# Turn-by-turn row halves for the scores and transposes of an RWKV-7 scan on Trainium2

## The chip, the cores and the metric

The kernel runs on one core of one Trainium2 chip. The metric is the device time of one execution in microseconds (us), as a median over runs. All arithmetic is in float32; the large products split each operand in a high and a low part, so that one dense product is three matrix instructions.

## What is computed

The reference is a decoder trunk of two layers on 1024 tokens of width 1024. Layer 0 mixes tokens with a gated linear recurrence, layer 1 with RWKV-7; behind each mixer stand a SwiGLU feed-forward part (22 tiles of 128 hidden units) and a gated embedding. The change lies in the RWKV-7 layer, whose heart is a state of 64 by 64 for each of 16 heads:

```python
def step(S, inp):
    r_t, w_t, k_t, v_t, a_t, b_t = inp
    sa = jnp.einsum('bhvk,bhk->bhv', S, a_t)
    S = S * w_t[:, :, None, :] + sa[..., None] * b_t[:, :, None, :] + v_t[..., None] * k_t[:, :, None, :]
    y = jnp.einsum('bhvk,bhk->bhv', S, r_t)
    return S, y
```

followed by a norm of each head's output, a bonus term, a gate and the output projection.

## The kernel before

The tokens are worked in two halves of 512. The recurrence above is done in chunks of 64 tokens (eight chunks per half), for pairs of heads: head 0 of a pair lies in partitions 0 to 63 (`E`), head 1 in 64 to 127 (`O`). There are 16 pair-halves (8 pairs, 2 halves of tokens), and two pairs make a group `G`, 8 groups in all.

`scan()` is made of four generators that run beside each other and beside the dense products of other stages:

- `stage1` builds, for each pair-half, the tiles `BK` (keys), `ZL` and `RB`; it forms the **scores** (`sc`) of four chunks at a time, so two rounds per pair-half, and then the **transposes** of `BK` into `BKt` (`bkt`, line 1079). A score product has 64 rows of contraction, 128 output partitions and 128 columns; a round has four of them for each head. VectorE masks each head's scores out of PSUM in three instructions (L1056 to L1058). ScalarE copies each head's transposes (L1082).
- `inverse` inverts the triangular matrices of a group (tiles `w`, `n`, `u`, `v`), by products on blocks that alternate between the upper and the lower partitions.
- `stage2` walks over the chunks of a group: `zu` and `y` products, of which those that read `z` and `V` (L1207) and those into `y` (L1223) also alternate between the two halves of the partitions, each half with its own half of the output partitions.
- `norm2` norms the outputs of a group, two pairs one behind the other (`bsum` at L1247, `yv` at L1254), loads the gate, and stores `o` (L1264). The two pairs of a group share two buffers of the tag `t3` (`bon` and `sq`): the second pair's loads wait until the first pair is through with them.

TensorE's order is fixed by hand while the scan runs. Every matrix instruction adds its estimated time to `self.clock` (`mm`, L114). After each dense product `tick` (L125) looks whether a generator may go on: each has yielded how long its operands will take (times `slack`, 3 in the first part and 2.5 at the end), whether it takes a PSUM bank, and what must have been traced before. The scan's rounds share `BANKS = 2` banks of tag `b`; `big` (L967) hands them out by turns, and `evac` notes at which planned time a bank will be free. Before the change each head's round takes one bank and is a step of its own, with a planned pause between the steps.

Where the dense products run out, `until` lets the scan run alone (L1352 to L1368): before the output projection of pairs 6 and 7 of the first half (`K.until(lambda: K.n2[3])`, L1360), and at the end, before the room of the scan is given to other tiles:

```python
    K.ffn(1, (0,), None, FA)
    K.until(lambda: not K.streams)
    c.close()
    extra(ctx)
```

The dense products have the names `pps` (projections), `pg` and `pu` (gate and up of the feed-forward part), `ops` (output projections: `ops<-hid` of the feed-forward part, `ops<-on` of the mixer). Their weights come by DMA into `raw`, are rounded by ScalarE (L237) and their rest is formed by GpSimd (L238), both into `whl`.

Of the kernel before, what the change touches and what calls it, by code (L numbers as in the profile page):

```python
# [25 lines left out]
# the plan of TensorE's order beside the scan: PSUM banks of the scan's rounds, the factor on  # L26
# its latencies with the pause behind each of its steps (ns) for either half, and how far the evacuations move ahead of what was traced before them.
# [26 lines left out]
class Part:  # L54
    def __init__(self, gen):
        self.gen, self.need = gen, (0.0, False, None)


class Kern:
# [47 lines left out]
    def ahead(self, n):  # L107
        """ahead of the n instructions traced before, where the scan runs beside dense products."""
        return self.tc.high_priority(n) if self.region else nullcontext()
# [11 lines left out]
    def ready(self, st):  # L121
        lat, bank, cond = st.need
        return (cond is None or cond()) and max(lat, self.bank_free[self.bank_n % BANKS] if bank else 0.0)

    def tick(self, wait=False):  # L125
        """lets each part of the scan whose operands should be there by now issue its next products."""
        while self.streams and (wait or self.clock >= self.hold):
            for st in self.streams:
                t = self.ready(st)
                if t is not False and t <= self.clock:  # L130
                    self.step(st)
                    break
            else:
                return
# [12 lines left out]
    def until(self, cond):  # L147
        """the scan alone until cond holds."""
        self.tick(True)
        while not cond():  # L150
            ts = [t for t in map(self.ready, self.streams) if t is not False]
            self.clock = max(self.clock, min(ts))
            self.tick(True)

    def pause(self, lat):
        """the dense products wait for other engines."""
        if self.streams:
            end = self.clock + lat
            while self.clock < end and self.streams:
                self.tick(True)  # L160
                ts = [t for t in map(self.ready, self.streams) if t is not False]
                self.clock = min([end] + [t for t in ts if t > self.clock])
# [6 lines left out]
    def ln_exp(self):  # L169
        """loads the one table that has both Ln and Exp, behind what ScalarE got up to here."""  # L170
        self.tc.keep_in_program_order(self.nc.scalar.preload_act_table_set("natural_log_exp_and_others"))

    def sigmoid(self, out, x, bias=None, nbias=None):
        """beside the scan without another table: exp(-ln(1 + exp(-x)))."""
        nc = self.nc
        if not self.region:
            nc.scalar.activation(out, x, AF.Sigmoid, **({} if bias is None else {"bias": bias}))
        else:
            nc.scalar.activation(out, x, AF.Exp, scale=-1.0, **({} if nbias is None else {"bias": nbias}))
            nc.scalar.activation(out, out, AF.Ln, bias=self.ones[: out.shape[0], 0:1])  # L180
            nc.scalar.activation(out, out, AF.Exp, scale=-1.0)

# [9 lines left out]
    def ps(self, nm):  # L192
        """a PSUM bank of a dense product."""
        if self.pe is not None:
            self.npe += 1
            if self.npe % 8 % 3:
                return self.pe.tile([128, TH], F32, tag="mm", name=nm, bufs=5)
        return self.pp.tile([128, TH], F32, tag="mm", name=nm, bufs=3)

    def xq(self, nm, ext=None):  # L200
        """8 KB: two k-tiles of half the tokens, hi and lo."""
        if ext is None:
            return self.xp.tile([128, 2, 2, TH], F32R, tag="xq", name=nm, bufs=6)
        return self.ep.tile([128, 2, 2, TH], F32R, tag=ext, name=nm, bufs={"xb": 4, "hid": 2}[ext])

    def ring(self, tag, shape, dt, bufs, more):
        """a slot of a ring, of the longer one while there is room for it."""
# [6 lines left out]
    def load_w(self, src, n, scale=None):  # L214
        """src: [128, n] float32 in DRAM -> f(part, a, b): columns a..b of the hi (0) or lo (1) part.

        scale: (factors [128, n / s / i, i], s), one for each s columns.
        """
# [26 lines left out]
    def mm3(self, *products):  # L245
        """(PSUM, list of (whi, wlo, xhi, xlo)): sums of products; of several ones with the first halves of the lists ahead."""
# [15 lines left out]
    def lead(self, tiles, n):  # L262
        """the first n tiles, whose operands may be on their way, beside each other; then one by one."""
        n = n if self.region else 1
        return [tiles[:n]] + [[i] for i in tiles[n:]]

    def halves(self, src, scale, xs, t, rows=128):
        """as wx for all k, with each 512 columns of the weights loaded when their products come."""
# [62 lines left out]
    def raw_x(self, k, t, gname, gi):  # L331
        """a tile of h times the gains; what divides by the norm stands behind the products with it."""
# [12 lines left out]
    def raw_norm(self, t, keep=True):  # L345
        """the norm for it, when the next products have begun."""
        def norm():
            self.rn[t] = self.rstd(t, self.acc[t] if keep else self.t2("rstd"))

        self.items = [lambda: None, norm]  # L350
# [9 lines left out]
    def order(self, n, tail, ts):  # L360
        """(tile, half): both halves of the first tiles, then half after half of the last ones."""
# [9 lines left out]
    def out_proj(self, wload, nk, hid, ts, bias=None, last=False, nxt=None, raw=None):  # L371
        """h += w @ hid; hid(k, t) -> (hi, lo)."""
# [25 lines left out]
    def hawk_consts(self):  # L398
# [15 lines left out]
        # 8 softplus(-lam) = 8 max(-lam, 0) + 16 atanh(e / (2 + e)); half of it, with either sign  # L414
# [17 lines left out]
    def hawk_tile(self, c, ts=(0, 1)):  # L432
# [6 lines left out]
        for t in ts:  # L439
# [23 lines left out]
            # sigmoid(x) = (1 + tanh(x / 2)) / 2  # L463
# [151 lines left out]
    def ple_last(self, l, t, ph, n=KD - 1):  # L615
        """the last tile of all, half after half of its columns, each up to the final norm."""
# [73 lines left out]
    def pre_rwkv(self, t):  # L690
        """keeps h in DRAM and normalizes it in place, its gains left to the mixes."""
# [15 lines left out]
    def xn_b(self, k0, k1):  # L707
        """the normalized tokens of half 1."""
# [7 lines left out]
    def half_b(self):  # L716
        """half 1 in the place of half 0."""
# [21 lines left out]
    def rwkv_proj(self, t):  # L739
# [13 lines left out]
        def shifted(cur, prev, p0, n, i):  # L753
            """cur + prev of the token before, normalized: products with (1 - mu) w and with mu w."""
# [83 lines left out]
        def unit(n, k):  # L838
            """k * k_k, of length 1 in each head."""
# [92 lines left out]
    def scan(self):  # L932
        """the scan of both halves, as parts that run beside each other and beside dense products.

        Each part yields (time until its next products' operands are there, whether these take a
        bank, what else has to be traced before them).
        """
# [36 lines left out]
        def evac():  # L974
            """called behind a round's products."""
# [13 lines left out]
        def stage1():  # L989
# [15 lines left out]
            for P, (t, g, jj) in enumerate(order):  # L1005
# [19 lines left out]
                # the slots of AB, ZL and RB are those of three pairs before  # L1025
# [3 lines left out]
                for c4 in range(0, NC, 4):  # L1029
# [18 lines left out]
                    yield 1500, True, None  # L1048
                    for hh, me, ot in HV:
                        ps = big("sc", 1700).rearrange("p (c s) -> p c s", c=4)  # L1050
                        for c in range(4):
                            self.mm(ps[:, c, :], BK[me, c4 + c, :, :].rearrange("p i s -> p (i s)"), zl[me, hh, c, :])
                        evac()
                        m3 = mask.unsqueeze(1).to_broadcast([128, 4, 128])
                        with self.ahead(AHEAD_S1):
# [3 lines left out]
                        if hh == 0:  # L1059
                            yield 0, True, None  # L1060
                yield 0, True, (lambda: (G == 0 or inv[G - 1] >= 1) and (old < 0 or s2[old] == NC))
# [13 lines left out]
                for hh, me, ot in HV:  # L1075
                    ps = c3(big("bkt", 800))
                    for c in range(NC):
                        nc.tensor.transpose(ps[:, c, :], BK[me, c, :, :].rearrange("p i s -> p (i s)"), ident[me])
                    self.clock += NC * 54
                    evac()  # L1080
                    with self.ahead(AHEAD_S1):
                        nc.scalar.copy(BKt[:, :, hh, :], ps)  # L1082
                    if hh == 0:
                        yield 0, True, None
# [12 lines left out]
        def inverse():  # L1097
            """(1 - A)^-1, A strictly triangular: blocks of 16 by substitution, then their products."""
# [189 lines left out]
    def rwkv_out(self, t, k0, k1, last=False, nxt=None, raw=None):  # L1288
        """h += w_o @ what tiles k0..k1 of the heads give."""
# [161 lines left out]
```

## Time and profile before

| what | us |
|---|---|
| median of 3 runs | 3109.62 |
| lowest and highest run | 3108.08, 3117.14 |
| span of the profiled execution | 3107.1 |
| TensorE busy in it | 2961.4 (95%) |
| VectorE, ScalarE, GpSimd busy | 1668.7, 1439.2, 1272.7 |

The profile gives the profiled execution no other time than its span, from its first to its last instruction; the median of the runs lies 2.5 us above it. The scan's products lie between 1131 and 2470 us. One float32 matrix instruction of the program shows as two records in the trace, each behind a record of its weight load; a transpose shows as one record. In the program order a row `sc ... x4` is therefore eight records.

### The profile page before, as it was taken

How to read it: one execution, taken by the hardware profiler on the slowest of the kernel's cores; microseconds unless marked ns; L12 is line 12 of the kernel's file. 1: busy time of each engine (PE TensorE's matmuls, PEld its weight loads, DVE VectorE, ACT ScalarE, POOL GpSimd, SP SyncE). 2: the span in 40 equal slices, each digit the busy share in tenths (PEclk: the TensorE clock that was granted, in tenths of full speed). 3: DMA queues.
4: the chain of work that ended last, by engine and by line, in shares of the span. 5: the costliest groups of instructions: out<-in, count | busy, mean ns of one | idle time of the engine just before them, and what ended most of it. 6: DMA issues, size and time to landing. Idle time of an engine off the chain costs nothing. (4 is left out here: it accounts for less than half of the span.)

```text
span 3107.1 us, 45858 instructions
## 1 busy us (share of the span) xinstructions
PE 2961.4 (95%) x16904; PEld 2290.3 (74%) x16904; DVE 1668.7 (54%) x2950; ACT 1439.2 (46%) x2565; POOL 1272.7 (41%) x1080
## 2 busy tenths in 40 slices
PE   5999999999999999999999899999999999999998
PEld 4777778888776777777776667777767777888886
DVE  8766671111563266565667665767866456222145
ACT  5564752222555443434455774454344445322244
POOL 5111134444445444443434334434333355544445
PEclk9999999999998999999999999999999999999999
DMA  3211123333335464333332457423323262333323
GB/s 122 64 36 53 50 82 102 95 95 95 99 124 176 157 193 129 87 110 89 100 108 89 141 174 212 132 85 111 101 88 101 70 185 87 104 96 95 95 81 109
DMA packets 223968, 336.04 MB, mean 108 GB/s; under 512 B 56960, under 2 KB 75136, under 8 KB 223744
## 3 DMA queue, kind: packets, MB, share of 16 engines
q1 hardware_dynamic: 223456, 332.75, 35.0%
q8 instruction: 133, 2.18, 0.3%
q14 instruction: 91, 0.75, 0.1%
q10 hardware_dynamic: 288, 0.37, 0.0%
HBM read 278.24 MB, written 54.79 MB: 107 GB/s over the span
## 5 line engine op out<-in xcount | busy, mean ns | idle before, releaser
L238 POOL TENSOR_TENSOR whl<-raw,whl 128x512 fp32r<-128x512 f32 (+2 forms) x818 | 1053.4, 1293 | 1441.8 <-ACT whl L237 1366.9
L237 ACT CAST whl<-raw 128x512 fp32r<-128x512 f32 (+2 forms) x818 | 482.2, 593 | 845.4 <-PE ops L115 228.7
L115 PE MATMUL ops<-hid,whl 128*128 128x512 f32 x2112 | 528.3, 403 | 19.2 <-ACT hid L288 7.8
L115 PE MATMUL pg<-xn,whl 128*128 128x512 f32 (+1 forms) x2184 | 526.0, 394 | 4.0 <-ACT whl L237 3.1
L115 PEld LDWEIGHTS ops<-hid,whl 128*128 128x128 f32 x2112 | 394.7, 191 | 120.5 <-DVE hid L289 12.9
L115 PEld LDWEIGHTS pg<-xn,whl 128*128 128x128 f32 x2184 | 405.8, 188 | 98.2 <-issue 4.4
L115 PE MATMUL pu<-xn,whl 128*128 128x512 f32 x1584 | 385.6, 396 | 2.7 <-ACT xn L288 1.4
L115 PEld LDWEIGHTS pu<-xn,whl 128*128 128x128 f32 x1584 | 296.0, 189 | 71.3 <-DVE xn L289 2.0
L115 PE MATMUL pps<-mix,whl 128*128 128x512 f32 x1152 | 301.8, 412 | 12.0 <-ACT mix L288 8.3
L389 DVE TENSOR_TENSOR h<-h,ops 128x512 f32<-128x512 f32 x256 | 174.1, 685 | 212.5 <-PE ops L115 210.6
L554 DVE TENSOR_TENSOR sg<-sg,pu 128x512 f32<-128x512 f32 x88 | 60.3, 685 | 404.4 <-PE pu L115 404.0
L115 PEld LDWEIGHTS pps<-mix,whl 128*128 128x128 f32 x1152 | 217.1, 193 | 75.6 <-ACT mix L288 10.3
L115 PE MATMUL pg<-raw,whl 128*128 128x512 f32 x720 | 199.7, 416 | 0.0
L115 PEld LDWEIGHTS pg<-raw,whl 128*128 128x128 f32 x720 | 133.7, 192 | 34.7 <-issue 4.1
L240 POOL TENSOR_SCALAR whl<-raw 128x512 fp32r<-128x512 f32 (+2 forms) x84 | 58.5, 701 | 216.4 <-PE rps L115 74.6
L115 PE MATMUL pu<-raw,whl 128*128 128x512 f32 x528 | 140.9, 406 | 0.0
L115 PE MATMUL rps<-xn,whl 128*128 128x512 f32 x480 | 123.0, 404 | 16.4 <-ACT xn L288 10.4
L115 PEld LDWEIGHTS rps<-xn,whl 128*128 128x128 f32 x480 | 91.9, 193 | 42.5 <-issue 12.0
L115 PE MATMUL gps<-xn,whl 128*128 128x512 f32 x480 | 118.4, 401 | 0.0
L115 PE MATMUL ops<-m,whl 128*128 128x512 f32 x480 | 114.4, 396 | 0.8 <-ACT m L288 0.8
L115 PEld LDWEIGHTS pu<-raw,whl 128*128 128x128 f32 x528 | 96.1, 188 | 23.4 <-issue 1.9
L115 PEld LDWEIGHTS gps<-xn,whl 128*128 128x128 f32 x480 | 92.4, 193 | 21.6 <-issue 0.5
(277 smaller groups left out, 4006.7 us busy)
## 6 DMA issues: line engine op xcount, KB each, us to landing
raw<-in_ffn_in SPq DMA_DIRECT2D x352, 256.0 KB, 2.6
raw<-in_ffn_out SPq DMA_DIRECT2D x152, 256.0 KB, 2.7
raw<-in_rkv SPq DMA_DIRECT2D x96, 256.0 KB, 3.1
raw<-in_ple_gate SPq DMA_DIRECT2D x64, 256.0 KB, 2.6
raw<-in_w_in SPq DMA_DIRECT2D x48, 256.0 KB, 2.8
h<-h SPq DMA_DIRECT2D x32, 256.0 KB, 3.3
raw<-in_ffn_out SPq DMA_DIRECT2D x48, 128.0 KB, 2.1
raw<-in_w_o SPq DMA_DIRECT2D x24, 256.0 KB, 2.7
```

Source lines behind the costliest of these rows:

```text
L115: self.nc.tensor.matmul(out, lhsT=lhsT, rhs=rhs, start=start, stop=stop)
L237: nc.scalar.copy(hl[:rows, 0, :w], raw[:rows, :w])
L238: nc.gpsimd.tensor_sub(hl[:rows, 1, :w], raw[:rows, :w], hl[:rows, 0, :w].bitcast(F32))
L240: nc.gpsimd.tensor_scalar(hl[:rows, 0, :w], raw[:rows, :w], 1.0, 0.0, ALU.mult, ALU.add)
L389: nc.vector.tensor_add(hs, hs, ps)
L554: nc.vector.tensor_mul(sg, sg, pu)
```

## The change

A generator may now ask for two banks at once: `need` holds a number, and `ready` waits until both of the next banks are free by the plan. In a round of scores both heads' banks are taken together, and the products go chunk by chunk, head 0 on the upper 64 rows of TensorE into one bank, head 1 on the lower 64 rows into the other. The plan's clock takes 200 ns off for each second product. Six VectorE instructions follow, in the order of before. The transposes are treated alike: sixteen in a burst, head by head in turn, into two banks, then two copies on ScalarE. No instruction is added or taken away. (Comment lines that go with it are left out.)

```diff
 class Part:
     def __init__(self, gen):
-        self.gen, self.need = gen, (0.0, False, None)
+        self.gen, self.need = gen, (0.0, 0, None)
...
     def ready(self, st):
         lat, bank, cond = st.need
-        return (cond is None or cond()) and max(lat, self.bank_free[self.bank_n % BANKS] if bank else 0.0)
+        return (cond is None or cond()) and max([lat] + [self.bank_free[(self.bank_n + i) % BANKS] for i in range(int(bank))])
...
-                    yield 1500, True, None
-                    for hh, me, ot in HV:
-                        ps = big("sc", 1700).rearrange("p (c s) -> p c s", c=4)
-                        for c in range(4):
-                            self.mm(ps[:, c, :], BK[me, c4 + c, :, :].rearrange("p i s -> p (i s)"), zl[me, hh, c, :])
-                        evac()
-                        m3 = mask.unsqueeze(1).to_broadcast([128, 4, 128])
-                        with self.ahead(AHEAD_S1):
+                    yield 1500, 2, None
+
+                    pss = [big("sc", e).rearrange("p (c s) -> p c s", c=4) for e in (1700, 3400)]
+                    for c in range(4):
+                        for hh, me, ot in HV:
+                            self.mm(pss[hh][:, c, :], BK[me, c4 + c, :, :].rearrange("p i s -> p (i s)"), zl[me, hh, c, :])
+                            if hh:
+                                self.clock -= 200
+                    evac()
+                    evac()
+                    m3 = mask.unsqueeze(1).to_broadcast([128, 4, 128])
+                    with self.ahead(AHEAD_S1):
+                        for hh, me, ot in HV:
+                            ps = pss[hh]
                             nc.vector.tensor_mul(AB[me, cs, :], ps[me, :, 0:64], m3[me, :, 0:64])
                             nc.vector.tensor_mul(rb[me], ps[me, :, 64:128], m3[me, :, 64:128])
                             nc.vector.tensor_mul(zl[ot, hh], ps[ot], m3[ot])
-                        if hh == 0:
-                            yield 0, True, None
-                yield 0, True, (lambda: (G == 0 or inv[G - 1] >= 1) and (old < 0 or s2[old] == NC))
+                yield 0, 2, (lambda: (G == 0 or inv[G - 1] >= 1) and (old < 0 or s2[old] == NC))
...
-                for hh, me, ot in HV:
-                    ps = c3(big("bkt", 800))
-                    for c in range(NC):
-                        nc.tensor.transpose(ps[:, c, :], BK[me, c, :, :].rearrange("p i s -> p (i s)"), ident[me])
-                    self.clock += NC * 54
-                    evac()
-                    with self.ahead(AHEAD_S1):
-                        nc.scalar.copy(BKt[:, :, hh, :], ps)
-                    if hh == 0:
-                        yield 0, True, None
+                pss = [c3(big("bkt", e)) for e in (800, 1400)]
+                for c in range(NC):
+                    for hh, me, ot in HV:
+                        nc.tensor.transpose(pss[hh][:, c, :], BK[me, c, :, :].rearrange("p i s -> p (i s)"), ident[me])
+                self.clock += NC * 60
+                evac()
+                evac()
+                with self.ahead(AHEAD_S1):
+                    for hh in range(2):
+                        nc.scalar.copy(BKt[:, :, hh, :], pss[hh])
```

Since the plan sets TensorE's order, the scan's steps move to other places among the dense products. Three places follow. The first is the start of the scan on TensorE: the scores of the first pair among the projections `pps` (and `vtr`, transposes of values). Before:

```order
L115 MATMUL pps<-mix,whl 128x512 x15
L115 MATMUL sc<-ZL,BK 128x128 x4
L115 MATMUL pps<-mix,whl 128x512 x6
L115 MATMUL sc<-ZL,BK 128x128 x4
L115 MATMUL pps<-mix,whl 128x512 x3
L115 MATMUL vtr<-cst,o 128x128 x4
L115 MATMUL pps<-mix,whl 128x512 x23
L115 MATMUL sc<-ZL,BK 128x128 x4
```

With the change:

```order
L115 MATMUL pps<-mix,whl 128x512 x15
L115 MATMUL sc<-ZL,BK 128x128 x8
L115 MATMUL pps<-mix,whl 128x512 x9
L115 MATMUL vtr<-cst,o 128x128 x4
L115 MATMUL pps<-mix,whl 128x512 x24
L115 MATMUL vtr<-cst,o 128x128 x4
L115 MATMUL pps<-mix,whl 128x512 x7
L115 MATMUL sc<-ZL,BK 128x128 x8
```

The four bursts of a pair-half's scores are two now, and the second comes 40 dense products and 8 `vtr` behind the first.

The second place is the output projection of the first half (`ops<-on`), on TensorE. Its first 144 products take heads 0 to 11 and its last 48 the heads 12 to 15, for each tile of outputs three products with pair 6 and then three with pair 7 (heads 14 and 15), which comes out of the last `yv` of group 3. Before, that `yv` stands in the middle of the projections `pps`, and `ops<-on` begins 128 products `pps` later:

```order
L115 MATMUL pps<-mix,whl 128x512 x8
L1078 MATMUL bkt<-cst,BK 128x64 x8
L115 MATMUL pps<-mix,whl 128x512 x6
L115 MATMUL yv<-v,cst 128x512
L115 MATMUL pps<-mix,whl 128x512 x8
L115 MATMUL vtr<-cst,o 128x128 x8
L115 MATMUL pps<-mix,whl 128x512 x24
```

With the change:

```order
L115 MATMUL yv<-v,cst 128x512
L115 MATMUL ops<-on,whl 128x512 x13
L115 MATMUL sc<-ZL,BK 128x128 x8
L115 MATMUL ops<-on,whl 128x512 x48
L1082 MATMUL bkt<-cst,BK 128x64 x16
L115 MATMUL ops<-on,whl 128x512 x18
L115 MATMUL bsum<-b,cst 128x512
L115 MATMUL ops<-on,whl 128x512 x26
L115 MATMUL yv<-v,cst 128x512
L115 MATMUL ops<-on,whl 128x512 x61
```

Group 3's last `yv` now stands behind 105 of the 144 products, with 39 of them left before the 48 (the 61 are these 39 and 22 of the 48).

The third place is the end of the scan: on TensorE, the last `y` and the norms of group 7. Before:

```order
L115 MATMUL y<-RB,SV 64x64 x4
L115 MATMUL pg<-raw,whl 128x512 x11
L115 MATMUL pu<-raw,whl 128x512 x24
L115 MATMUL pg<-raw,whl 128x512 x2
L115 MATMUL bsum<-b,cst 128x512
L115 MATMUL pg<-raw,whl 128x512 x22
L115 MATMUL yv<-v,cst 128x512
L115 MATMUL pu<-raw,whl 128x512 x24
L115 MATMUL pg<-raw,whl 128x512 x24
L115 MATMUL pu<-raw,whl 128x512 x12
L115 MATMUL bsum<-b,cst 128x512
```

With the change:

```order
L115 MATMUL ops<-hid,whl 128x512
L115 MATMUL zu_8241<-z,V 64x64 x2
L115 MATMUL zu_8242<-z,V 64x64 x2
L115 MATMUL y<-RB,SV 64x64 x4
L115 MATMUL bsum<-b,cst 128x512
L115 MATMUL yv<-v,cst 128x512
L115 MATMUL bsum<-b,cst 128x512
L115 MATMUL yv<-v,cst 128x512
L115 MATMUL pu<-raw,whl 128x512 x24
L115 MATMUL pg<-raw,whl 128x512 x48
```

The dense products of the stage `FA` are used up before the scan is done, so its last six steps stand behind each other with nothing between. On the DMA queue of SyncE the weights of the `pg` products then stand behind the last store of the scan (these rows are of the change):

```order
L1264 DMA v<-g_390 128x512
L1268 DMA o_406<-ys 128x512
L226 DMA raw<-in_ffn_in 128x512 x2
L1281 DMA h_22146<-h_248 128x512
L1281 DMA h_22146<-h_250 128x512
```

Before, that store was issued while `ops<-hid` of the stage `FA` still ran on TensorE.

## Rows read from the trace of the kernel before

**Rows 1.** The page's first line.

```profile
span 3107.1 us, 45858 instructions
```

**Rows 2.** Windows, the scan: length, five engines' busy us (count), PEclk, DMA, GB/s.

```profile
1131.00:2470.00 1339.00, 1277.25 (x9796) 954.07 (x9795) 878.44 (x1876) 649.11 (x1322) 528.41 (x428) 0.97 0.38 116
```

**Rows 3.** By tile, the scores: duration ns min/median/max, first and last start.

```profile
L115 PE MATMUL sc<-ZL,BK x512: 271/272/579, 1131.9 to 2360.0; 64*128 64x128 f32 x171
L1056 DVE TENSOR_TENSOR AB<-sc,cst x64: 392/419/429, 1133.1 to 2360.3; 64x256 f32<-64x256 f32 x64
...
L1058 DVE TENSOR_TENSOR ZL<-sc,cst x64: 676/689/695, 1133.8 to 2361.1; 64x512 f32<-64x512 f32 x64
```

**Rows 4.** By tile, the transposes.

```profile
L1078 PE MATMUL bkt<-cst,BK x256: 221/222/274, 1149.8 to 2365.9; 64*128 64x64 f32 x128
```

**Rows 5.** Timeline, TensorE: start us, us, instruction; two bursts of scores.

```profile
1131.88 1.16 PE L115 MATMUL sc<-ZL,BK 64*128 64x128 f32 x8
1132.96 1.66 PE L115 MATMUL pps<-mix,whl 128*128 128x512 f32 x6
1134.56 1.16 PE L115 MATMUL sc<-ZL,BK 64*128 64x128 f32 x8
```

**Rows 6.** Timeline, TensorE: two bursts of transposes.

```profile
1149.79 0.71 PE L1078 MATMUL bkt<-cst,BK 64*128 64x64 f32 x8
1150.42 2.11 PE L115 MATMUL pps<-mix,whl 128*128 128x512 f32 x8
1152.47 0.71 PE L1078 MATMUL bkt<-cst,BK 64*128 64x64 f32 x8
```

**Rows 7.** Timeline, TensorE: a long run of dense products.

```profile
2504.67 20.10 PE L115 MATMUL ops<-hid,whl 128*128 128x512 f32 x86
```

**Rows 8.** Timeline of 60 ns: the first two records of an alternating burst.

```profile
1277.45 0.27 PE L115 MATMUL zu<-z,V 64*64 64x64 f32 x2
```

**Rows 9.** Timeline of 150 ns: the first two records of one score product.

```profile
1131.88 0.48 PE L115 MATMUL sc<-ZL,BK 64*128 64x128 f32 x2
```

**Rows 10.** Timeline, all engines: the last steps of the scan.

```profile
2466.62 0.45 PE L115 MATMUL zu<-z,V 64*64 64x64 f32 x8
...
2467.24 0.37 DVE L1210 COPY SV<-zu 64x64 f32<-64x64 f32 x2 [0.25 <-ACT SV L1209]
...
2498.33 1.02 PE L115 MATMUL bsum<-b,cst 128*128 128x512 f32 x2
...
2499.39 0.69 DVE L1250 SCALAR_TENSOR_TENSOR b<-bsum,v 128x512 f32<-128x512 f32 x1
...
2500.11 0.63 ACT L1251 ACTIVATE v<-ys 128x512 f32<-128x512 f32 x1 [0.41 <-DVE b L1250]
...
2504.22 1.02 PE L115 MATMUL yv<-v,cst 128*128 128x512 f32 x2
...
2510.04 0.76 DVE L1263 TENSOR_TENSOR ys<-ys,v 128x512 f32<-128x512 f32 x1 [0.34 <-DMA v<-g]
...
2512.40 0.38 SPq L1264 DMA_DIRECT2D o<-ys  x1
```

**Rows 11.** DMA issues: KB each, median us from issue to landing.

```profile
v<-v SPq DMA_DIRECT2D x16, 256.0 KB, 3.5
...
o<-ys SPq DMA_DIRECT2D x16, 256.0 KB, 3.1
...
on<-o SPq DMA_DIRECT2D x16, 256.0 KB, 3.9
```

**Rows 12.** By tile, the operand of the output projection.

```profile
L288 ACT CAST on<-on x16: 613/619/624, 1894.5 to 2543.3; 128x512 fp32r<-128x512 f32 x16
```

**Rows 13.** Timeline, TensorE: its longest wait in the scan.

```profile
2263.55 2.05 PE L115 MATMUL bsum<-b,cst 128*128 128x512 f32 x2 [6.22 <-issue]
```

**Rows 14.** Windows behind that wait, columns as in rows 2.

```profile
2263.00:2266.00 3.00, 2.44 (x4) 0.88 (x4) 2.94 (x6) 0.58 (x2) 3.00 (x3) 0.50 0.33 87
2266.00:2270.00 4.00, 4.00 (x14) 3.39 (x14) 2.64 (x5) 0.63 (x1) 0.05 (x1) 0.50 0.38 131
```

## The prediction

> **What bounds the kernel.** I read the windows first: over the whole scan, from 1131 to 2470 us, TensorE is busy 1277 of 1339 us at a mean granted clock of 0.97, while VectorE is at 878 and GpSimd at 528 [rows 2]. So time on TensorE is what counts there: the scan's products and the dense ones share one queue, and what a burst takes is taken from the dense products. The views by tile then give what is edited: 512 records of scores, 256 of transposes [rows 3, 4]. The sum of their durations is no price, since records overlap (the ends are modelled). The price of a burst is read in the timeline: from the start of one burst to the start of the next, less the dense products between. A dense product takes 0.234 us: 86 of them in 20.10 us [rows 7]. Two bursts of scores start 2.68 us apart with six dense products between: 2.68 - 6 x 0.234 = **1.28 us a burst** [rows 5]. Two of transposes start 2.68 us apart with eight between: 2.68 - 8 x 0.234 = **0.81 us** [rows 6]. These include the way into the burst and out of it, which the records hide.
>
> **Merging and interleaving the bursts.** Within a burst, records follow each other at (1.16 - 0.48) / 6 = 0.113 us for scores, the 0.48 being the first two [rows 5, 9]; for transposes, (0.71 - 0.27) / 7 = 0.063, with a first record of 0.27 as in the other bursts of 64 columns [rows 6, 8]. So a single score burst is 8 x 0.113 = 0.90 us of stream and 0.38 of entry and exit; a transpose burst is 0.50 and 0.31. What do two halves cost in turn? The trace does not show row halves that share their output columns. The nearest row is the burst into `zu` from `z` and `V`, which alternates between halves that differ in rows and in columns: its first two records both lie within 0.27 us, the length of one [rows 8], whereas two records of one score product reach over 0.48 [rows 9]. There the second half is free. The bounds are therefore:
> - All overlaps: a pair of bursts costs as much as one burst did. 32 rounds of scores save 1.28 each, 41.0 us; 16 of transposes save 0.81, 13.0 us; together **54.0 us**.
> - None overlaps: only one entry and exit is saved, 32 x 0.38 + 16 x 0.31 = **17.1 us**.
> - A loss is excluded for the burst itself: the records are the same, with one entry fewer.
>
> I take 54.0, because the row of the alternating burst is nearest: same number format, same 64 rows, halves told apart by the same starting partitions.
>
> The Trainium skill, page "TensorE: Matmul & The Clock Gate", section "Part 3: Packing small matmuls — row/col tiling", gives a measured 3.07 for four row tiles. By that share of 0.77, an estimate from the page, two halves would be worth 1.54, a pair of records would cost 1.3 times one, and about 11 us of the saving would be lost.
>
> VectorE's masks and ScalarE's copies are the same instructions as before and cost nothing while TensorE has dense products in front of it; six masks now stand together, 2 x (0.42 + 0.42 + 0.69) = 3.1 us (the third kind, RB, has AB's shape) [rows 3]. The price if that cover is gone is the second rival.
>
> **What moves: the end of the scan.** The order shows that stage 1, asking for two banks, falls behind, and the scan no longer ends inside the dense products of `FA`. Its last steps then wait on each other with TensorE idle. From the last steps of before, now laid end to end [rows 10]:
> - `z` copied, `z,V`, its copies into `SV`, `y`: from `z,V` to the end of the copy is 2467.61 - 2466.62 = 1.0 us; twice that, and 0.4 for `y`: 2.4.
> - `bsum` to the end of the square on ScalarE: 2500.74 - 2498.33 = 2.4.
> - first `yv` to the last multiplication of that pair: 2510.80 - 2504.22 = 6.6; only then is the buffer free into which the second pair's `v` is loaded, 3.5 [rows 11]; the masked sum and square, 2500.74 - 2499.39 = 1.35; second `yv` 0.45.
>
> That is 16.7 us, in which TensorE does about 2.6 us of work that it did before too: 14.1 us exposed. Then the weights of `pg`: their loads stand behind the last store of `o`, which is issued 2512.40 - 2504.22 = 8.2 us behind its `yv`; a load of the same size takes 3.5 [rows 11] and the cast 0.62 [rows 12], so 12.3 us, of which `yv` and 24 products `pu` cover 0.45 + 24 x 0.234 = 6.1: 6.2 exposed. **Tail: 20.3 us.**
>
> **What moves: the first output projection.** The last `yv` of group 3 now has 39 dense products before those that need its heads, and three more before the first that must wait: 0.45 + 42 x 0.234 = 10.3 us of cover. The chain is 8.2 to the store [rows 10], 3.1 for the store to land, 3.9 for the load [rows 11], 0.62 for the cast [rows 12]: 15.8. Exposed: 5.5 us. After a wait of 6.2 us the granted clock stands at 0.50 for the next 7 us [rows 13, 14], the 1.2 GHz level, which takes 3.5 us more. **Stall: 9.0 us.** In the tail the slow clock falls on `pu`, inside the wait for `pg`, and is counted already.
>
> **Sum.** 3107.1 [rows 1] - 54.0 + 20.3 + 9.0 = 3082.4 for the span. The median of the runs lies 2.5 above the profiled span, so **3085 us**. About 0.3% (9 us) is what a measurement of this kernel can tell from no change.
>
> **Rivals.**
> - *The halves do not overlap at all.* For: they share the output columns, which no alternating burst of before does. Against: they write different banks, and the records of the two halves alternate one by one, as in the burst that does overlap. Then 3109.6 - 17.1 + 29.3 = **3122 us, slower**. It decides where the saving falls under the 29.3 us of stalls, that is where less than a third of the stream of 36.9 us (54.0 - 17.1) is won.
> - *They overlap in part.* Half of the stream: 3109.6 - 35.6 + 29.3 = 3103 us. The skill's share above would give 3096, an estimate from that page.
> - *The evacuation becomes the wait.* Both banks are filled at once, and the second bank's masks end 1.5 us later than before [rows 3]. Whoever takes a bank next (transposes, inverse, norms) may reach TensorE's head first and hold up the dense products behind it. Once per pair-half, 16 x 1.5 = 24 us: 3109 us. Against: the plan allows 1700 and 3400 ns, times a slack of 2.5 to 3, for these banks, and in the trace the longest wait of the scan is one for loads, not for a bank [rows 13]. The skill's page "TensorEngine Tiling (Array Packing)", section "PSUM Bottleneck", says that tiling speeds up the products but not the copies out of PSUM, which may become the bound; no run here shows it yet.
> - *The stalls stay half hidden*, because queues run ahead of what I assumed: 3085 - 15 = 3070 us.
> - *The edit does not interleave*: excluded, the order shows `x8` and `x16` in place of two bursts.
>
> **Chances.** Forecast 0.57, no overlap 0.09, part overlap 0.09, evacuation 0.16, stalls half hidden 0.09. The range from 3066 to 3111 holds the forecast with its spread of some 12 us, the part overlap, the half hidden stalls and most of the evacuation case, and leaves out the case without overlap. Faster by over 0.3% (below 3100.3) takes 0.54 of the forecast, 0.09 of the hidden stalls and 0.06 of the two cases near 3103 and 3109: 0.69. Within 0.3%: 0.22, mostly the evacuation case and the part overlap. Slower: 0.09, mostly no overlap.
>
> **What would show it.** Right: two records of scores within 0.27 to 0.3 us at a burst's head; a burst of sixteen score records that costs about 1.3 us of TensorE's time by the same reading; TensorE waits of 10 to 17 us in all at the last `bsum` and `yv`, then one on the weights of `pg`; one of some 6 us in `ops<-on` of the first half, on the cast of `on`; the granted clock at 0.50 behind each. Wrong: records of the two halves 0.11 us apart (no overlap), or waits of `bkt`, `w` or `n` on VectorE's masks that were not there before (evacuation), or a span outside 3064 to 3109.

## The result, and the profile after

The kernel with the change takes 3140.94 us in the median of four runs (3139.36 to 3144.2), the kernel before, measured beside it, 3108.85 us. The ratio is 1.0097, with a 95% interval from 1.008 to 1.0113: **slower by 1%**, where 3085 us was forecast, and outside the range of 3066 to 3111. The profiled span went from 3107.1 us [rows 1] to 3139.8, by 32.7 us.

The page of the changed kernel, its first lines:

```profile
span 3139.8 us, 45863 instructions
...
PE 2934.1 (93%) x16904; PEld 2267.1 (72%) x16904; DVE 1689.0 (54%) x2950; ACT 1437.8 (46%) x2565; POOL 1283.5 (41%) x1080
```

TensorE is less busy than before (2961.4 us there), and the kernel is longer. The windows over the scan say where (columns as in rows 2). The first line is the stretch of rows 2; the second goes from the first scores to the end of the last `ops`, the last output projection that runs beside the scan:

```profile
1131.00:2470.00 1339.00, 1229.49 (x9409) 924.12 (x9408) 883.28 (x1810) 637.69 (x1281) 539.10 (x430) 0.96 0.39 117
```

```profile
1134.64:2532.45 1397.81, 1288.30 (x10000) 967.03 (x10000) 910.41 (x1887) 664.38 (x1347) 556.77 (x443) 0.96 0.38 115
```

The second stretch in the kernel before:

```profile
1131.88:2524.61 1392.73, 1330.98 (x10024) 997.37 (x10024) 905.23 (x1911) 673.74 (x1363) 557.29 (x449) 0.97 0.39 117
```

TensorE's idle time in the scan was 1339.0 - 1277.2 = 61.8 us [rows 2]; now it is 1339.0 - 1229.5 = 109.5. In the longer stretch TensorE is busy for 42.7 us less and idle for 47.8 more, so the stretch is 5.1 us longer, with 24 of its records moved out behind it. The last `ops` ends 7.8 us later, since the first scores already start 2.8 us later. The other 25 us or so of the 32.7 come behind the last `ops`, in the tail.

**The bursts do what was forecast.** Timeline of TensorE in the changed kernel, two bursts of scores and one of transposes (columns as in rows 5):

```profile
1200.70 1.16 PE L115 MATMUL sc<-ZL,BK 64*128 64x128 f32 x16
1201.80 3.70 PE L115 MATMUL ops<-hid,whl 128*128 128x512 f32 x15
1205.33 5.60 PE L115 MATMUL pg<-xn,whl 128*128 128x512 f32 x24
1210.77 2.20 PE L115 MATMUL pu<-xn,whl 128*128 128x512 f32 x9
1212.90 1.16 PE L115 MATMUL sc<-ZL,BK 64*128 64x128 f32 x16
...
1225.11 0.71 PE L1082 MATMUL bkt<-cst,BK 64*128 64x64 f32 x16
1225.74 3.70 PE L115 MATMUL pu<-xn,whl 128*128 128x512 f32 x15
1229.28 5.60 PE L115 MATMUL pg<-xn,whl 128*128 128x512 f32 x24
```

Sixteen records last 1.16 us, as eight did [rows 5]; sixteen transposes last 0.71, as eight did [rows 6]. The price, with a dense product at (1210.77 - 1205.33) / 24 = 0.227 us, is 1212.90 - 1200.70 - 48 x 0.227 = 1.3 us for both heads; rows 5 give by the same 0.227 a price of 2.68 - 6 x 0.227 = 1.3 for one. The second head is free. The share that the prediction took from the 3.07 for four tiles in the Trainium skill ("TensorE: Matmul & The Clock Gate", "Part 3: Packing small matmuls — row/col tiling") does not hold for these two halves.

**TensorE's waits** from 1131 to 2540 us, before (us in total, times, longest):

```profile
PE bsum L115 <- issue: 12.5, 3, 6.2
PE zu L115 <- DVE ys L1232: 6.7, 5, 3.8
PE ops L115 <- DVE sg L553: 4.1, 1, 4.1
PE yv L115 <- ACT v L1251: 4.0, 1, 4.0
```

and after:

```profile
PE bsum L115 <- DMA b<-b: 12.5, 2, 12.3
PE sc L115 <- DVE b L1254: 9.0, 3, 6.6
PE ops L115 <- ACT hid L288: 8.4, 3, 4.0
PE ops L115 <- ACT on L288: 7.0, 1, 7.0
PE zu L115 <- DVE SV L1214: 6.9, 6, 2.0
PE yv L115 <- ACT v L1255: 6.2, 2, 4.8
PE bkt L1082 <- DVE b L1254: 5.5, 2, 4.0
```

No single wait holds the loss: scores and transposes now wait for the norm (14.5 us), dense products for their operands, steps of the scan for the steps before them. The longest wait is on the load of `b` for the second pair of a norm, in the middle of the scan:

```profile
1801.49 2.05 PE L115 MATMUL bsum<-b,cst 128*128 128x512 f32 x2 [12.27 <-DMA b<-b]
```

The kernel before already had waits at the scan's two banks. Its three waits of `bsum`, for which the profile names no releaser (`issue`, 12.5 us), each end 0.10 us behind a mask of the scores. At the longest one, where `bsum` starts at 2263.55 us [rows 13], that mask is:

```profile
2262.76 0.69 DVE L1058 TENSOR_TENSOR ZL<-sc,cst 64x512 f32<-64x512 f32 x1
```

The load of `b`, the only one that this `bsum` reads, had been issued at 2251.94 us, and no transfer of `b` in the scan takes longer than 5.4 us to land. By these times the norm stood behind the masks before, and scores and transposes stand behind the norm now, for about as long.

**The tail** (timeline from the last `ops` on; TensorE, and of the others what ends its waits):

```profile
2532.02 0.50 PE L115 MATMUL ops<-hid,whl 128*128 128x512 f32 x1
2532.45 0.45 PE L115 MATMUL zu<-z,V 64*64 64x64 f32 x8
2533.09 0.94 PE L115 MATMUL y<-RB,SV 64*64 64x64 f32 x8 [0.19 <-ACT SV L1213]
2533.96 1.13 PE L115 MATMUL bsum<-b,cst 128*128 128x512 f32 x2
2536.54 1.12 PE L115 MATMUL yv<-v,cst 128*128 128x512 f32 x2 [1.46 <-ACT v L1255]
2544.13 2.05 PE L115 MATMUL bsum<-b,cst 128*128 128x512 f32 x2 [6.47 <-DMA b<-b]
2548.39 2.07 PE L115 MATMUL yv<-v,cst 128*128 128x512 f32 x2 [2.21 <-ACT v L1255]
2551.24 7.21 PE L115 MATMUL pu<-raw,whl 128*128 128x512 f32 x24 [0.78 <-ACT v L1261]
2561.74 1.19 PE L115 MATMUL pg<-raw,whl 128*128 128x512 f32 x2 [3.29 <-DMA raw<-in_ffn_in]
```

In the order of before, 227 dense products of the stage still stand behind the last `y` of the scan; in the new one none does. That count tells, for each kernel below, how far the plan pushed the scan back.

### The profile page after: what moved, and what is told of

Its sections match the earlier page's. It is cut to its first block, busy times and chain, and to the rows that moved or that the text cites. A ratio compares the mean times of both kernels' runs of the same rounds, so it can differ in the third digit from the quotient of the medians.

```text
span 3139.8 us, 45863 instructions
## 1 busy us (share of the span) xinstructions
PE 2934.1 (93%) x16904; PEld 2267.1 (72%) x16904; DVE 1689.0 (54%) x2950; ACT 1437.8 (46%) x2565; POOL 1283.5 (41%) x1080
## 5 line engine op out<-in xcount | busy, mean ns | idle before, releaser
L115 PE MATMUL pps<-mix,whl 128*128 128x512 f32 x1152 | 307.5, 417 | 10.2 <-ACT mix L288 4.3
L289 DVE TENSOR_TENSOR hid<-sg,hid 128x512 fp32r<-128x512 f32 x88 | 89.2, 1013 | 47.0 <-ACT hid L288 46.8
```

Of the source, the lines that this page charges most:

```text
L115: self.nc.tensor.matmul(out, lhsT=lhsT, rhs=rhs, start=start, stop=stop)
L289: (nc.gpsimd if pool else nc.vector).tensor_sub(lo, src, hi.bitcast(F32))
```

## The experiments

Two theories stood against each other at first. *Displaced order*: a round that asks for two banks, with long estimates of when they come free, pushes the scan's steps back, and the steps meet where nothing covers them. *The norm's bank*: the scores' second bank is still held by `bsum` (released by VectorE, L1254), and TensorE's queue stands still until then. Behind both is the question of what TensorE's time is worth here.

### e1: the overlap taken away, the order kept

```diff
-                    for c in range(4):
-                        for hh, me, ot in HV:
+                    for hh, me, ot in HV:
+                        for c in range(4):
```

and the same two lines for the transposes.

> The changed kernel took 3141 us. Here each burst issues head 0's products first and then head 1's, into the same two banks; TensorE's order of bursts among the dense products is the changed kernel's. If the overlap of the row halves works and TensorE's time is what counts, the lost overlap costs 32 x 8 x 0.113 + 16 x 8 x 0.063 = 37 us: 3178, and a score burst costs 2.2 us instead of 1.29. If most bursts stand next to waits that would absorb them, the loss is under 20 us: below 3160.

Measured: 3153.37 us, ratio to before 1.0136 [1.0117, 1.0156]. The same 48 dense products lie between the same two bursts (timeline of e1):

```profile
1198.33 1.71 PE L115 MATMUL sc<-ZL,BK 64*128 64x128 f32 x16
...
1211.09 1.71 PE L115 MATMUL sc<-ZL,BK 64*128 64x128 f32 x16
...
1223.85 1.01 PE L1082 MATMUL bkt<-cst,BK 64*128 64x64 f32 x16
1224.79 3.70 PE L115 MATMUL pu<-xn,whl 128*128 128x512 f32 x15
1228.33 5.60 PE L115 MATMUL pg<-xn,whl 128*128 128x512 f32 x24
```

The two bursts start 12.76 us apart in place of 12.20: 0.56 us for a round of scores; 4.48 in place of 4.17, 0.31, for one of transposes. That is 32 x 0.56 + 16 x 0.31 = 23 us of TensorE's time, where 37 were expected. The kernel became 12.4 us longer (the profiled span 7.7), below 3160 as the second expectation had it. So the overlap is real, and about half of what it saves never reaches the end.

### e2: a denser second half of the scan

```diff
-PACE = ((3, 1200), (2.5, 200))
+PACE = ((3, 1200), (2, 200))
```

> The change, with the plan's factor on latencies 2 instead of 2.5 in the last part (from the second output projection of the first half on). The scan's last norm then stands 160 dense products before the end of FA instead of behind it. If the exposed tail is worth what I read in the changed kernel's timeline (16 us to the last yv, 5 for the weights of pg, 3 of slow clock), 3141 - 24 = 3117. If the steps, standing closer, wait on each other instead, the gain is under 10 us: above 3131.

Measured: 3126.36 us, 1.005 [1.0031, 1.0068]; 275 dense products are left behind the last `y`. The tail is gone, some 15 us come back, 9 fewer than the first expectation had; the time lies between the two. The waits of the scan are not gone (its largest two, 1131 to 2540 us):

```profile
PE bsum L115 <- DMA b<-b: 17.8, 3, 13.3
PE sc L115 <- DVE b L1254: 12.5, 4, 5.5
```

### e3: shorter estimates for the two banks

```diff
-                    pss = [big("sc", e).rearrange("p (c s) -> p c s", c=4) for e in (1700, 3400)]
+                    pss = [big("sc", e).rearrange("p (c s) -> p c s", c=4) for e in (1000, 1700)]
```

> The change, with the plan's time to a free bank behind the scores 1000 and 1700 ns instead of 1700 and 3400. Stage 1 is then not held back: the yv of group 3 stand at 6516 and 6610 dense products (before: 6532 and 6656; changed: 6816 and 6921), but the last one still at the end of FA. Theory of displaced order (the waits come because the scan ran late in the plan): the stall at the output projection goes (10 us) and half of the other new waits (25): 3141 - 35 = 3106. Rival (two banks at once make TensorE wait for whoever holds the second bank): more waits of sc and bkt on the masked sum of the norm, 3141 or more.

Measured: 3109.24 us, 0.9994 [0.9983, 1.0004]: 32 us below the change, with two numbers of the plan and no instruction altered; 139 dense products are left at the end. The waits for the norm's bank did not shrink (14.3 us in front of scores, 14.5 us in all with the change):

```profile
PE sc L115 <- DVE b L1254: 14.3, 3, 5.9
PE nps L115 <- DVE acc L300: 10.0, 1, 10.0
PE yv L115 <- ACT v L1255: 8.5, 3, 4.0
```

So the order costs these 32 us, and the norm's bank is not what costs them. About half of the gain lies in the tail, where the end of one pair's norm is left instead of two norms: from the end of the last `ops` to the end of the kernel the profiled execution takes 590.7 us, where the change takes 607.4 and the kernel before 582.5.

### e4: a long estimate for the norm's bank

```diff
-                    bs = big("bsum", 900)
+                    bs = big("bsum", 4000)
```

> The change, with the plan's time to a free bank behind the norm's first product (bsum) 4000 ns instead of 900. Bank theory: the 16 us of waits of sc and bkt on the norm's masked sum go, with some 8 us of slow clock behind them; the last yv of group 3 moves from 6921 to 6960 dense products, which lengthens the stall at the output projection by 39 x 0.234 = 9 us: 3141 - 24 + 9 = 3126. Theory of displaced order: no gain, 3141 to 3150.

Measured: 3160.07 us, 1.0158 [1.014, 1.0176], above both expectations. The plan now keeps scores and transposes away from that bank, and waits on `b L1254` are gone from the list; others took their place (1131 to 2540 us):

```profile
PE yv L115 <- ACT v L1255: 28.2, 6, 7.7
PE nps L115 <- DVE acc L300: 14.9, 3, 6.8
PE gx L115 <- DVE whl L822: 11.1, 2, 10.0
```

The norm's bank as the only cause falls. What is pushed back further costs more.

### e5 and e6: one half of the change alone

e5 has the scores of the change and the transposes of before, e6 the reverse:

```diff
-                pss = [c3(big("bkt", e)) for e in (800, 1400)]
-                for c in range(NC):
-                    for hh, me, ot in HV:
...
+                for hh, me, ot in HV:
+                    ps = c3(big("bkt", 800))
+                    for c in range(NC):
```

> Only the scores are paired; the transposes are two bursts in one bank each, as in the kernel before. The last yv of group 3 stands at 6875 dense products (before 6656, changed 6921), the last of all at 8449 with one pair behind the end of FA. If TensorE's own time decides, the 16 transposes' pairs cost 16 x 0.81 = 13 us again: 3141 + 13 = 3154. If the place of the scan's steps decides, the shorter tail and the earlier norms give back more than that: 3115 to 3135.

Measured: 3126.38 us, 1.0056 [1.0039, 1.0073], within the second expectation; 108 dense products left.

> Only the transposes are paired; scores as before. The steps stand near those of the kernel before (last yv of group 3 at 6679, last of all at 8449 with one pair behind FA). TensorE saves 13 us. Theory of displaced order: 3110 - 13 + about 10 for the half of the tail = 3107, some us more for new waits. Bank theory: a pair's transposes wait for both banks 16 times, no gain: 3115 to 3125.

Measured: 3126.96 us, 1.0061 [1.0046, 1.0076]; 126 left. e5 saves some 41 us of bursts and e6 some 13, and they take the same time: the amount saved does not set it. e6 lies 20 us above the first of its expectations and 2 above the range of the bank theory, and its two longest sums of waits are for the norm's bank, 28.5 us (1131 to 2540 us):

```profile
PE sc L115 <- DVE b L1250: 19.4, 4, 8.1
PE bkt L1078 <- DVE b L1250: 9.1, 1, 9.1
```

So in e6's order the bank does cost time. Both kernels also share half a tail: one pair's norm ends behind the last `ops`, and from there to the end they take 593.0 and 592.0 us, some 10 more than the kernel before.

### e7: e2 and e3 together

> Shorter bank estimates and the faster end together: last yv of group 3 at 6610, last of all at 8165 (before 8363). Alone they took 32 and 15 us off the changed kernel. Theory of displaced order: both together, 3109 - 15 = 3094. Rival (what TensorE saves is eaten by waits wherever the steps stand): 3105 to 3115.

Measured: 3099.36 us, 0.9972 [0.9957, 0.9987], faster than either kernel and between its two expectations; 396 dense products left. The half tail that e3 still had is gone: from the last `ops` to the end it takes 577.5 us, 13.2 less than e3, of 15.1 us between their profiled spans. As in e3, the gain over the change comes from the order alone, 41.6 us by now.

### e8: e7, with the norm in banks of the dense products

```diff
-                    yield (Y1 if jj else 3000), True, None
-                    bs = big("bsum", 900)
+                    yield (Y1 if jj else 3000), False, None
+                    bs = self.ps("bsum")
...
-                    evac()
```

and likewise for `yv`.

> As the run with both estimates and the faster end, and the norm's two products take a bank of the dense products' ring instead of the scan's two, so that a pair of scores never waits for the norm's masked sum. Bank theory: the 14 us of waits of sc and bkt on that sum go, with some 5 of slow clock: 3094 - 19 = 3075. If the wait moves to the dense products, which now share the ring: 3090 to 3100.

Measured: 3094.56 us, 0.9958 [0.9941, 0.9974], the best with e11. The second expectation is met. The waits of scores and transposes for the norm are gone (7.3 us were left of them in e7), for some 5 us, a quarter of the 19 that the theory of the norm's bank gave; the intervals of e7 and e8 overlap, so these 5 us are not clear of noise. The scan ends in time: its TensorE runs through where the tail of the change stood.

```profile
2495.64 18.92 PE L115 MATMUL ops<-hid,whl 128*128 128x512 f32 x82 [1.50 <-ACT hid L288]
2514.40 5.76 PE L115 MATMUL pg<-raw,whl 128*128 128x512 f32 x24
```

The first `pg` starts 10.2 us ahead of the one before (2524.61).

### e9 and e10: what TensorE's time is worth in a good order

e9 is e8 with the loops of e1 (no overlap). e10 is the kernel before with e8's norm and e2's pace: single bursts, and about as many dense products left behind the scan (478, against 435 in e8 and e9).

> The same three edits of the order's numbers as e8 (3094.56 us) and the same bursts at the same places, but the products of head 0 stand ahead of those of head 1 in each burst, so that the halves of TensorE do not work beside each other; e1 showed that this costs 0.54 us in a burst of scores and 0.30 us in one of transposes, 32 x 0.54 + 16 x 0.30 = 22 us of TensorE's time. If TensorE's own time sets the scan's stage in this order, 3094.6 + 22 = 3116 us. If much of it still disappears in waits for the vector engines, as in the order of the change (22 us became 12), about 3094.6 + 8 to 12 = 3103 to 3107 us. If the overlap is worth nothing in time, 3095 us.

Measured: 3101.43 us, 0.9978 [0.9966, 0.999], between the second and the third expectation.

> The kernel before (one head's burst at a time, one bank each) with the two edits of e8 that it can take: the norm of the heads in banks of the dense products' ring, and a factor of 2 in place of 2.5 on the latencies of the second half of the scan. It tells whether e8's gain belongs to the bursts or to the order's numbers alone. If the bursts of two heads bring the gain once their order is mended, this stays with the kernel before, 3105 to 3115 us (it has no stall at the norm's bank to take away, and its scan already ended in time). If the order's numbers alone bring it, 3090 to 3098 us. If a denser second half costs as it did in e2 (28 us between two landmarks), 3115 to 3130 us.

Measured: 3120.38 us, 1.0043 [1.0027, 1.006], as the third expectation had it. Windows from the first scores to the end of the last `ops` of e10, e9 and e8, one after the other (columns as in rows 2):

```profile
1131.31:2538.30 1406.99, 1337.06 (x10025) 1000.14 (x10024) 910.43 (x1907) 671.82 (x1359) 560.80 (x451) 0.97 0.38 117
```

```profile
1132.42:2520.95 1388.53, 1309.17 (x10024) 985.70 (x10024) 915.33 (x1899) 672.43 (x1359) 559.57 (x449) 0.97 0.39 119
```

```profile
1132.69:2514.40 1381.71, 1296.84 (x10024) 969.17 (x10024) 911.17 (x1899) 670.81 (x1359) 563.06 (x449) 0.96 0.39 120
```

From e10 to e8 the bursts lose the whole 54 us and the time falls by 25.8 us; the first step, one burst in place of two, gives 19 of them, the overlap (23 us of TensorE's time) gives 6.9. The rest goes two ways. Idle time grows at each step, 69.9, 79.4, 84.9 us, by 15 in all. And TensorE's busy time falls by 40.2 us only: 13.8 us of the 54 are busy time again, at a granted clock of 0.96 in e8 against 0.97 in e10. The clock is of the size to explain it (0.01 of 1400 us is 14, from rounded shares). The difference between e9 and e8 is about as large as their intervals; e1 shows the same sign with 12.4. Only e9 and e8 have one order: the steps of e10 stand at places of their own.

### e11: both halves of the scan denser

```diff
-PACE = ((3, 1200), (2, 200))
+PACE = ((2.5, 1200), (2, 200))
```

> As e8 (3094.56 us), and also a factor of 2.5 in place of 3 on the latencies of the first half of the scan: its steps come earlier beside the dense products. If the scan's steps still come late at the end and hold the output projection up, some 5 to 10 us less than e8, 3085 to 3090 us. If what is left is waits for the vector engines at steps that come too early, later than e8, 3100 to 3115 us.

Measured: 3094.07 us, 0.9957 [0.994, 0.9974]: no difference from e8. The waits moved to the scores (13.3 us for the masks of the round before, VectorE L1064, where e8 has 4.2 in the scan). Neither expectation was met.

### e12: the kernel before, with the norm off the banks

> The kernel before with one edit of e8 alone: the norm of the heads in banks of the dense products' ring, the pace of the scan as it was. In e10 the same edit with a denser second half gave 3120.4 us, 10.5 us over the kernel before of the same call. If the denser half is what costs there (as in e2), this is at the kernel before, 3106 to 3112 us, and the gain of e8 (15 us) needs the bursts of two heads. If the norm's bank was worth 5 us here too (as from e7 to e8), 3104 us. If the norm in the dense ring holds the dense products up, about 3118 us, and it is this edit that costs in e10.

Measured: 3111.82 us, 1.0 [0.9989, 1.0012]. So it is the denser second half that costs e10 its time (8.6 us more than e12), and e8's gain over the kernel before does not come from the norm's edit alone. The expectation of e10 said that the kernel before has no stall at the norm's bank, which is so for the scores only: its `bsum` waited 12.5 us for masks there. e12 has 4.7 us of waits in front of `bsum`, none of them on a mask, and gains nothing by it.

## Why the prediction was wrong

- **The price of the bursts and the full overlap: right.** Both heads cost what one did, 54 us of TensorE's time in all. The bound without overlap was mis-sized: 0.90 us of stream for the second head's scores, where e1 shows 0.56 (0.31 for transposes in place of 0.50). A burst's way in and out is then about 1.3 - 0.56 = 0.7 us, not 0.38; merging alone was worth 54 - 23 = 31 us of TensorE's time, not 17.1. Two records of scores at a burst's head lie within 0.38 us, not 0.27 to 0.3, but one alone takes 0.37 there.
- **The step that failed is the first term of the sum, 3107.1 - 54.0**, and under it the sentence that time on TensorE "is what counts there". 1277 us busy of 1339 [rows 2] was read as a bound. It is a share: it says that TensorE had little slack in that order, not that what it saves comes off the end. At equal order about a third to a half does: of the overlap's 23 us, 12.4 in e1 and 6.9 in e9. Of the 54 us, 25.8 come off from e10 to e8, but e10 has a poor order for single bursts (8.6 us above e12); against the kernel before, e8 is 14.4 us faster. The rest turned into waits and, by the granted clock, into slower work. The forecast allowed for 9.0 us of that in the scan, 5.5 of wait and 3.5 of slow clock. From the first scores to the last `ops` the change shows 47.8 us more of idle time, and 54.0 + 2.6 - 42.7 = 13.9 us of the saving (2.6 being the work moved behind) are busy time again, at a granted clock of 0.96 in place of 0.97.
- **The order's new places were counted at two spots only.** That stage 1 falls behind was in the prediction, but its cost was worked out for the tail and one output projection, 29.3 us. The wait of 12.27 us at 1801 us is a third spot; e3 and e7 do not have it. By the runs the order costs 32 us (e3's two numbers) to 41.6 (e7's three). This is the smaller part of the miss: with the order of e7 the same instructions are 9.6 us faster than the kernel before, where the first term has 54.0. By e7, of the 56 us between forecast and time some 12 (41.6 - 29.3) belong to the order and some 44 (54.0 - 9.6) to the first term.
- **The tail: right in kind and nearly in size.** 20.3 us of exposure and 2.6 of work moved there make 22.9; the last `ops` ends 7.8 us late and the kernel 32.7, so the tail is some 25. The wait on the second pair's loads (6.47), on the square (2.21) and on the weights of `pg` (3.29) are the ones named; as in the forecast, the clock falls in it (0.75 from 2532 to 2563 us).
- **The first output projection: right.** 7.0 us on the cast of `on`, against 5.5, and then 16 products in 6.95 us at a granted clock of 0.54, where full speed takes 16 x 0.227 = 3.6: 3.3 us against the 3.5 forecast. Timeline of TensorE there:

```profile
2012.31 6.95 PE L115 MATMUL ops<-on,whl 128*128 128x512 f32 x16 [6.98 <-ACT on L288]
```

- **"The evacuation becomes the wait" was near, but not it.** The prediction set it aside because the longest wait of the scan is "one for loads, not for a bank" [rows 13]. That reading was wrong: that wait ends with a mask of the scores (L1058), some 6 us after the load must have landed. With the change a wait for a bank did appear in front of scores and transposes, 14.5 us, in the way that rival described. The bank was not held by masks, though, but by the norm's sum, whose VectorE instruction comes late. The timeline at the longest of these waits:

```profile
2170.79 0.69 DVE L1254 SCALAR_TENSOR_TENSOR b<-bsum,v 128x512 f32<-128x512 f32 x1
...
2171.54 1.86 PE L115 MATMUL sc<-ZL,BK 64*128 64x128 f32 x13 [6.57 <-DVE b L1254]
```

Scores start 0.06 us behind the end of L1254. A request for two banks waits for the later of them. That head 0's scores would have gone ahead with one bank each is not shown: in e6 the single bursts wait 19.4 us for the same sum. Taking the norm away from the banks gave some 5 us, not clear of noise (e8), and nothing in the kernel before (e12), so this wait is a part, not the cause.

What stays open: why the share is what it is, and which engine sets the end of the scan in the good order. No run took work from VectorE or ScalarE, and none held the clock. That a denser second half gains e7 10 us has a plain reason, the half tail that e3 still had and the kernel before has not. Why it costs e10 9 us is not settled, nor why e6's order meets the norm's bank so often. Each order has its own collisions, and the runs show their sum.

## What to carry to other kernels

A busy share of 95% does not mean that TensorE's savings come off the end in full. Where several engines hand steps to each other, price the saving by a kernel with the same order and the saving taken away (here loops exchanged, 23 us of work for 7 to 12 us of time). A change that asks for a resource in a larger unit moves everything that a planner orders by that resource; look first where the last step of the chain stands against the work that should cover it, and set the planner's estimates anew before judging the change. With three numbers and the norm's bank set anew, the same edit goes from 1% slower to 0.4% faster.

## What the runs showed of the hardware

Products on the two row halves of TensorE, with all 128 output columns in common but into two banks, overlap fully when issued turn by turn: sixteen records in 1.16 us, as long as eight. Issued head by head, the second eight add 0.55 us (1.71), which is less than the 0.90 of stream that the pitch of 0.113 us within one head had suggested.
